# Expert stage of a hybrid encoder block: place of the scales' copy, of the one-hots and of the first weight splits

## The chip, the cores and the metric

One core of one Trainium2 chip. The time is device microseconds of one execution. TensorE multiplies, VectorE and ScalarE work on elements, GpSimd does as well and issues indirect transfers, SyncE issues the weight loads; each of them works through its own instructions in a fixed order.

## The reference

One layer over 1024 tokens of 1024 channels: windowed attention and gated linear attention, then an expert layer, then a gated embedding and a last norm. The change touches the expert layer alone:

```python
def expert_choice_ffn(xn, w_router, w_gate, w_up, w_down):
    B, S, D = xn.shape
    cap = CAPACITY_FACTOR * S // N_EXPERTS
    aff = jax.nn.softmax(jnp.einsum('bsd,de->bse', xn, w_router).astype(jnp.float32), axis=-1)
    top_aff, top_idx = lax.top_k(jnp.swapaxes(aff, 1, 2), cap)
    bidx = jnp.arange(B)[:, None, None]
    xg = xn[bidx, top_idx]
    hid = jax.nn.silu(jnp.einsum('becd,edf->becf', xg, w_gate)) * jnp.einsum('becd,edf->becf', xg, w_up)
    y = jnp.einsum('becf,efd->becd', hid, w_down) * top_aff[..., None].astype(xn.dtype)
    return jnp.zeros((B, S, D), dtype=y.dtype).at[bidx, top_idx].add(y)
```

16 experts, each takes its 128 best tokens of 1024 and runs them through three matrices of 1024x1024 in float32: 12 MB of weights per expert.

## The kernel before

Every product is made of three: a float32 is split into a high part (a cast to float32r on ScalarE) and a low part (what the cast left, a subtraction on VectorE), and TensorE adds high x high, high x low and low x high (`split`, line 105, and the three matmuls at lines 1198 to 1200).

Before the experts come a router and a sort. For each of the eight token tiles, affinities to the 16 experts are computed; VectorE finds the 128 largest of every expert with max and replace steps (lines 916, 918) and merges sorted halves with pairs of max and min (lines 935, 936). From the threshold follows `posT`, each token's place among the expert's 128.

`tokens(e)` (line 1119) turns the places into a list: VectorE compares `posT` with a row of numbers, which gives the one-hots `oh` (line 1121), TensorE multiplies them with the token numbers (line 1125), VectorE adds two columns into `idx` (line 1127). `gather(e)` has GpSimd issue an indirect transfer that brings the 128 rows of `xn_d` into `xg` (line 1133); each row carries 1024 normed channels and 17 scales (16 affinities and the norm's factor). There is one buffer `xg`.

`begin(e)` copies the scales of `xg` into `col` on ScalarE (line 1214) and has TensorE turn the rows, two groups of four transposes (line 1178), which are split into `xt_h` and `xt_l`. `gate`, `up` and `down` each consist of four quarters (`quarter_of`): a piece of 1 MB of weights arrives in one of 15 raw buffers, is split into `hi` and `lo` (called `slot` in the profile; three pairs of buffers in all), and is multiplied by 12 matmuls. `gate` ends with a SiLU on ScalarE (line 1229), `up` with a product on VectorE (line 1238), both scaled by `col`; `down` ends with `y`, scaled on ScalarE (line 1255), which GpSimd adds to `h_d` with an indirect transfer (line 1256).

The experts are staggered: while expert e goes through gate and up, the hidden rows of e − 1 are turned inside its gate (`hidden_turned`), and the down product of e − 1 comes after its up. After the first quarter of that down, `ahead(e + 1)` begins expert e + 1, gathers e + 2 and finds the list of e + 3. Before the loop, lists 0, 1 and 2 and the gathers 0 and 1 are written down first. The first two pieces have their lo half made by GpSimd; their splits are put behind an instruction of the lists, `found`, and one of the router, `placed`, each on its own engine.

The order of work on each engine comes from the program's scheduler, which starts from the order of writing and moves instructions by its own estimate of when they are ready. Three things bind it: data and buffers; `on_pe`, which keeps the transposes and expert products of TensorE in the order of writing (the products with one-hots are not bound so); and `tc.issue_after(ins)`, which puts what is written in its block behind `ins` on the engine of `ins`.

## Time and profile before

| | us |
|---|---|
| median of 3 runs | 1800.95 (1798.8 to 1804.61) |
| profiled execution | 1803.04, its span 1801.3 |
| TensorE busy in the span | 1676.5 (93%) |
| VectorE busy | 1207.0 (67%) |
| ScalarE busy | 898.5 (50%) |
| GpSimd busy | 204.4 (11%) |
| of these, line 106 on weight pieces (`slot`): VectorE, the lo halves | 433.0 |
| line 106 on weight pieces: ScalarE, the hi halves | 373.9 |

The sort and the lists reach to about 1050 us of the span, the experts from there to about 1680, and the last part to its end. A row of a timeline gives start, length, engine, line, operation, output and inputs, and in brackets how long the engine had been idle and what ended that. A matmul's row overlaps with the next one's, so twelve of 0.39 us take less than twelve times that.

### The profile page before, as it was taken

What the parts mean: (1) busy time and instruction counts of PE and PEld (TensorE: products, weight loads), DVE (VectorE), ACT (ScalarE), POOL (GpSimd) and SP (SyncE); (2) the same over time, 40 slices, a digit from 0 to 9 for tenths busy, and PEclk for the clock granted to TensorE, in tenths of its full rate; (3) what the DMA queues carried; (4) which work ended last, traced back from release to release, by engine and by line L of the source; (5) the groups of instructions that cost most, each with busy time, mean ns of one, the idle gap of its engine ahead of it and who ended that gap; (6) DMA issues with size and microseconds to landing.
All of it is one profiled execution on the core that took longest, in us unless ns stands there. A gap on an engine that the chain in (4) does not pass through costs nothing.

```text
span 1801.3 us, 23090 instructions
## 1 busy us (share of the span) xinstructions
PE 1676.5 (93%) x8795; PEld 1370.3 (76%) x8795; DVE 1207.0 (67%) x2254; ACT 898.5 (50%) x1259; POOL 204.4 (11%) x199
## 2 busy tenths in 40 slices
PE   7998999999999999999988769999999998889997
PEld 6977766768898989888866557777777776677786
DVE  7446754633746473743577968888888887778575
ACT  4345555432626262530322336777677776667642
POOL 1013300000000000000143310111111111101000
PEclk9999999999999999999988979999999999999999
DMA  6032410524221211164423869999999998882811
GB/s 223 1 101 106 129 47 24 164 69 153 61 68 51 71 48 47 51 230 143 174 94 118 320 244 359 354 369 376 377 347 365 372 358 325 315 308 93 291 47 47
DMA packets 123607, 335.06 MB, mean 186 GB/s; under 512 B 9180, under 2 KB 41988, under 8 KB 123496
## 3 DMA queue, kind: packets, MB, share of 16 engines
q1 hardware_dynamic: 106784, 277.96, 42.7%
q0 software_dynamic: 14704, 53.17, 8.7%
q10 hardware_dynamic: 2008, 2.46, 0.4%
q8 instruction: 69, 1.13, 0.3%
q14 instruction: 42, 0.34, 0.1%
HBM read 290.50 MB, written 43.06 MB: 185 GB/s over the span
## 4 chain that ended last, share of the span: by engine, by line
PE 56%; issue 26%; DVE 9%; POOL 3%; DMA 3%; ACT 2%; DVEq 0%; POOLq 0%; SPq 0%; ACTq 0%
PE ps_mm L111 12%; PE ps_mm L109 11%; PE ps_mm L110 11%; PE ps_b L109 2%; PE ps_b L111 2%; PE ps_b L110 2%; POOL h_d L1256 2%; POOL xg L1133 1%; DMA xg<-xn_d,idx 1%; PE ps_b L1199 1%; DVE rs_y L133 1%; PE ps_b L1200 1%; PE ps_b L1198 1%; PE ps_a L533 1%; PE ps_tr L562 1%
## 5 line engine op out<-in xcount | busy, mean ns | idle before, releaser
L106 DVE TENSOR_TENSOR slot<-slot 128x2048 fp32r<-128x2048 f32 (+1 forms) x191 | 433.0, 2284 | 108.0 <-ACT slot L106 105.1
L106 ACT CAST slot<-slot 128x2048 fp32r<-128x2048 f32 (+1 forms) x200 | 373.9, 1875 | 118.4 <-PE ps_b L1199 44.6
L111 PE MATMUL ps_mm<-aT_h,wl 128*128 128x512 f32 x512 | 204.4, 399 | 0.0
L109 PE MATMUL ps_mm<-aT_h,wh 128*128 128x512 f32 x512 | 203.1, 397 | 1.2 <-ACT sgr L246 1.2
L110 PE MATMUL ps_mm<-aT_l,wh 128*128 128x512 f32 x512 | 203.8, 398 | 0.0
L1199 PE MATMUL ps_b<-slot,xt_h 128*128 128x512 f32 x256 | 103.3, 403 | 15.0 <-DVE slot L106 15.0
L1199 PE MATMUL ps_mm<-slot,xt_h 128*128 128x512 f32 x256 | 102.7, 401 | 13.6 <-DVE slot L106 13.6
L109 PEld LDWEIGHTS ps_mm<-aT_h,wh 128*128 128x128 f32 x512 | 97.4, 190 | 18.8 <-ACT sgr L246 1.5
L111 PEld LDWEIGHTS ps_mm<-aT_h,wl 128*128 128x128 f32 x512 | 97.5, 190 | 18.3 <-issue 1.2
L110 PEld LDWEIGHTS ps_mm<-aT_l,wh 128*128 128x128 f32 x512 | 97.2, 190 | 18.4 <-issue 1.2
L1198 PE MATMUL ps_mm<-slot,xt_h 128*128 128x512 f32 x256 | 103.3, 404 | 5.3 <-ACT slot L106 3.9
L1198 PE MATMUL ps_b<-slot,xt_h 128*128 128x512 f32 x256 | 102.8, 402 | 5.5 <-ACT slot L106 5.5
L106 DVE TENSOR_TENSOR wl<-raw,wh 128x2048 fp32r<-128x2048 f32 (+1 forms) x29 | 61.5, 2122 | 65.0 <-ACT wh L106 65.0
L1200 PE MATMUL ps_b<-slot,xt_l 128*128 128x512 f32 x256 | 102.0, 398 | 0.0
L1200 PE MATMUL ps_mm<-slot,xt_l 128*128 128x512 f32 x256 | 101.5, 396 | 0.0
L106 ACT CAST wh<-raw 128x2048 fp32r<-128x2048 f32 (+1 forms) x30 | 52.0, 1735 | 93.5 <-PE ps_mm L110 88.7
L109 PE MATMUL ps_mm<-wh,aT_h 128*128 128x256 f32 x320 | 91.7, 287 | 0.8 <-DVE sgr L588 0.8
L111 PE MATMUL ps_mm<-wh,aT_l 128*128 128x256 f32 x320 | 90.6, 283 | 1.6 <-DVE aT_l L106 1.6
L110 PE MATMUL ps_mm<-wl,aT_h 128*128 128x256 f32 x320 | 90.7, 284 | 0.0
L109 PE MATMUL ps_mm<-slot 128*128 128x512 f32 x192 | 80.1, 417 | 0.0
L111 PE MATMUL ps_mm<-slot 128*128 128x512 f32 x192 | 77.8, 405 | 0.0
L110 PE MATMUL ps_mm<-slot 128*128 128x512 f32 x192 | 77.5, 404 | 0.0
(392 smaller groups left out, 3924.7 us busy)
## 6 DMA issues: line engine op xcount, KB each, us to landing
slot<-in_w_exp_gate_dram SPq DMA_DIRECT2D x64, 1024.0 KB, 7.9
slot<-in_w_exp_down_dram SPq DMA_DIRECT2D x64, 1024.0 KB, 7.6
slot<-in_w_exp_up_dram SPq DMA_DIRECT2D x60, 1024.0 KB, 5.7
raw<-in_w_in_dram SPq DMA_DIRECT2D x16, 1024.0 KB, 6.8
raw<-in_w_in_dram SPq DMA_DIRECT2D x14, 512.0 KB, 5.3
sg_d<-sgr POOLq DMA_DIRECT2D x14, 512.0 KB, 2.9
xn_d<-xa POOLq DMA_DIRECT2D x8, 520.5 KB, 3.8
xt<-in_x_dram SPq DMA_DIRECT2D x8, 512.0 KB, 7.0
```

The lines of the kernel that those rows point to most:

```text
L106: return nc.scalar.copy(hi, src), eng.tensor_sub(lo, src, hi)
L109: nc.tensor.matmul(out_ps, sh, mh, start=start, stop=False)
L110: nc.tensor.matmul(out_ps, sh, ml, start=False, stop=False)
L111: nc.tensor.matmul(out_ps, sl, mh, start=False, stop=stop)
L133: eng.scalar_tensor_tensor(y, t, c, y, op0=ALU.add, op1=ALU.mult)
L533: nc.tensor.matmul(pss[g][:, 0:n], qhl[r, g, hc], kT_l[r, ks], start=False, stop=False)
L562: nc.tensor.transpose(pt[:, o:o + 128], sm[g][c][:, j * 128:(j + 1) * 128], ident)
L1133: return nc.gpsimd.indirect_dma_start(out=xg, out_offset=None, in_=xn_d[:, :], in_offset=bass.IndirectOffsetOnAxis(ap=st[e]["idx"][:, 0:1] ...
L1198: on_pe(nc.tensor.matmul(po[c], src[0][:, kk], hi[:, k, cc], start=first, stop=False))
L1199: on_pe(nc.tensor.matmul(po[c], src[0][:, kk], lo[:, k, cc], start=False, stop=False))
L1200: on_pe(nc.tensor.matmul(po[c], src[1][:, kk], hi[:, k, cc], start=False, stop=last))
L1256: nc.gpsimd.indirect_dma_start(out=h_d[:, :], in_=y, in_offset=None, compute_op=ALU.add, out_offset=bass.IndirectOffsetOnAxis(ap=s["idx"][ ...
```

## The change

`begin` writes the copy of scales behind the splits of the turned rows, and puts it behind the second cast on ScalarE. The lists and the gather of expert 1 and the list of expert 2 are written behind the first quarter of the first gate, the list of expert 1 behind the first piece's lo half on VectorE. From expert 1 on, the list of e + 2 is written after the second quarter of the up product of e. Expert 1 is begun after the third quarter of the first up product. The last hidden rows are turned inside the down product of expert 14. The lo halves of the first pieces are made by VectorE, and the first three pieces (before: two) have their splits behind `found` and `placed`; `found` is now the index of expert 0 (before: of expert 1).

```diff
@@ -1134,12 +1134,8 @@
             out=xg, out_offset=None, in_=xn_d[:, :],
             in_offset=bass.IndirectOffsetOnAxis(ap=st[e]["idx"][:, 0:1], axis=0)).ins
 
-    for e in range(2):
-        found = tokens(e)
-        if e == 0:
-            gathered = gather(0)
-    gather(1)
-    tokens(2)
+    found = tokens(0)
+    gathered = gather(0)
 
 
     for i in range(4):
@@ -1177,7 +1173,7 @@
         for c in range(4):
             on_pe(nc.tensor.transpose(pt[:, c * 128:(c + 1) * 128],
                                       src[:, (g * 4 + c) * 128:(g * 4 + c + 1) * 128], ident))
-        split(th[:, g * 4:g * 4 + 4], tl[:, g * 4:g * 4 + 4], pt.rearrange("p (c t) -> p c t", c=4))
+        return split(th[:, g * 4:g * 4 + 4], tl[:, g * 4:g * 4 + 4], pt.rearrange("p (c t) -> p c t", c=4))
 
     def quarter_of(po, src, w, q):
 
@@ -1186,10 +1182,10 @@
             raw = loaded(next_pool(), (2, D), w[q * 256:q * 256 + 256], nc.gpsimd if 12 <= n < 16 else nc.sync)
         hi, lo = [slot(rawE if n % 3 == 2 else whl, (2, D), F32R) for _ in range(2)]
         with ExitStack() as es:
-            if n < 2:
+            if n < 3:
                 for ins in (found, placed):
                     es.enter_context(tc.issue_after(ins))
-            split(hi, lo, raw, nc.gpsimd if n < 2 else nc.vector)
+            lo_ins[0] = split(hi, lo, raw)[1].ins
         for k in range(2):
             kk = 2 * q + k
             for c in range(2):
@@ -1202,7 +1198,7 @@
     def hl_pair(po, name, **kw):
         return [po.tile([128, KC, 128], F32R, name=name + x, **kw) for x in ("_h", "_l")]
 
-    n_banks = [0]
+    n_banks, lo_ins = [0], [None]
 
     def two_banks():
         n_banks[0] += 1
@@ -1211,9 +1207,11 @@
     def begin(e):
         st[e]["xt"] = hl_pair(e2, "xt")
         col = st[e]["col"] = eg.tile([128, NE + 1], F32, name="col", bufs=NE)
-        nc.scalar.copy(col, st[e]["xg"][:, D:TW])
         for g in range(2):
-            turned(st[e]["xg"], *st[e]["xt"], g, "a")
+            here, _ = turned(st[e]["xg"], *st[e]["xt"], g, "a")
+
+        with tc.issue_after(here.ins):
+            nc.scalar.copy(col, st[e]["xg"][:, D:TW])
 
     def gate(e, after):
 
@@ -1228,11 +1226,13 @@
             cc = slice(c * 512, c * 512 + 512)
             nc.scalar.activation(s["hid"][:, cc], pg[c], AF.Silu, scale=s["col"][:, NE:NE + 1])
 
-    def up(e):
+    def up(e, after):
         s = st[e]
         pu = two_banks()
         for q in range(4):
             quarter_of(pu, s["xt"], w_eu[e], q)
+            if q in after:
+                after[q]()
         for c in range(2):
             cc = slice(c * 512, c * 512 + 512)
             nc.vector.scalar_tensor_tensor(s["hid"][:, cc], pu[c], s["col"][:, NE:NE + 1], s["hid"][:, cc],
@@ -1256,24 +1256,30 @@
         nc.gpsimd.indirect_dma_start(out=h_d[:, :], in_=y, in_offset=None, compute_op=ALU.add,
                                      out_offset=bass.IndirectOffsetOnAxis(ap=s["idx"][:, 0:1], axis=0))
 
+    def tokens_of(e, after=None):
+        if e < NE:
+            with tc.issue_after(after) if after else ExitStack():
+                tokens(e)
+
     def ahead(e):
 
         if e < NE:
             begin(e)
         if e + 1 < NE:
             gather(e + 1)
-        if e + 2 < NE:
-            tokens(e + 2)
+
+    def first_tokens():
+        tokens_of(1, lo_ins[0])
+        gather(1)
+        tokens_of(2)
 
     begin(0)
     for e in range(NE):
-        gate(e, {1: partial(hidden_turned, e - 1)} if e else {})
-        up(e)
+        last = {1: partial(hidden_turned, e)} if e == NE - 1 else {}
+        gate(e, {1: partial(hidden_turned, e - 1)} if e else {0: first_tokens})
+        up(e, {1: partial(tokens_of, e + 2)} if e else {2: partial(ahead, 1)})
         if e:
-            down(e - 1, {0: partial(ahead, e + 1)})
-        else:
-            ahead(1)
-    hidden_turned(NE - 1)
+            down(e - 1, {0: partial(ahead, e + 1), **last})
     down(NE - 1, {})
 
 
```

How that moves instructions, at three places. ScalarE around the start of an expert in the middle of the stage; `slot` is the hi half of a weight piece, `xt_h` the turned rows, `y` the result of the down product of another expert. Before:

```order
L106 CAST slot<-slot 128x2048 x5
L106 CAST xt_h<-ps_a 128x512 x2
L106 CAST slot<-slot 128x2048
L1214 COPY col<-xg 128x17
L106 CAST slot<-slot 128x2048
L1255 ACTIVATE y<-ps_mm,col 128x512
L106 CAST slot<-slot 128x2048
L1255 ACTIVATE y<-ps_mm,col 128x512
L106 CAST slot<-slot 128x2048 x2
```

After:

```order
L106 CAST slot<-slot 128x2048 x5
L106 CAST xt_h<-ps_a 128x512 x2
L1214 COPY col<-xg 128x17
L106 CAST slot<-slot 128x2048 x2
L1255 ACTIVATE y<-ps_b,col 128x512
L106 CAST slot<-slot 128x2048
L1255 ACTIVATE y<-ps_b,col 128x512
L106 CAST slot<-slot 128x2048 x2
L106 CAST hT_h<-ps_tr 128x512 x2
```

The copy stood one piece behind the casts of the turned rows, and it was the copy for the expert after, whose rows had just been asked for; now it stands right behind the casts and reads the rows that these casts came from.

VectorE at the end of the sort, from the places to the first expert's rows; `oh` and `idx` are one-hots and list of an expert, `slot` here is the lo half of a weight piece. Before:

```order
L1114 TENSOR_TENSOR posT<-sl_9694,sl_9695 128x128
L1121 TENSOR_TENSOR oh<-posT,iot 128x1024
L1127 TENSOR_SCALAR idx<-ps_a 128x1
L1121 TENSOR_TENSOR oh<-posT,iot 128x1024
L1127 TENSOR_SCALAR idx<-ps_a 128x1
L1121 TENSOR_TENSOR oh<-posT,iot 128x1024
L1127 TENSOR_SCALAR idx<-ps_a 128x1
L1121 TENSOR_TENSOR oh<-posT,iot 128x1024
L106 TENSOR_TENSOR xt_l<-ps_a,xt_h 128x512 x2
L106 TENSOR_TENSOR slot<-slot 128x2048 x7
```

After:

```order
L1114 TENSOR_TENSOR posT<-sl_9694,sl_9695 128x128
L1121 TENSOR_TENSOR oh<-posT,iot 128x1024
L1127 TENSOR_SCALAR idx<-ps_a 128x1
L106 TENSOR_TENSOR slot<-slot 128x2048
L1121 TENSOR_TENSOR oh<-posT,iot 128x1024
L106 TENSOR_TENSOR slot<-slot 128x2048
L106 TENSOR_TENSOR xt_l<-ps_a,xt_h 128x512
L106 TENSOR_TENSOR slot<-slot 128x2048
L106 TENSOR_TENSOR xt_l<-ps_a,xt_h 128x512
L1127 TENSOR_SCALAR idx<-ps_a 128x1
L1121 TENSOR_TENSOR oh<-posT,iot 128x1024
L106 TENSOR_TENSOR slot<-slot 128x2048
```

Behind the first list there stood two more lists and a one-hot, and the lo halves of pieces 0 to 2 had been made elsewhere; now these three halves stand between the lists and the two low parts of the turned rows.

GpSimd at the same place; `slot` at line 106 is the lo half of a piece, at line 813 the load of a piece of the second up product. Before:

```order
L1052 DMA xn_d<-xa 128x1041
L106 TENSOR_TENSOR slot<-slot 128x2048 x2
L1133 DMA xg<-xn_d,idx 128x1041
L813 DMA slot<-in_w_exp_up_dram 128x2x1024
L1133 DMA xg<-xn_d,idx 128x1041
L813 DMA slot<-in_w_exp_up_dram 128x2x1024 x3
```

After:

```order
L1052 DMA xn_d<-xa 128x1041
L1133 DMA xg<-xn_d,idx 128x1041
L813 DMA slot<-in_w_exp_up_dram 128x2x1024 x3
L1133 DMA xg<-xn_d,idx 128x1041
L813 DMA slot<-in_w_exp_up_dram 128x2x1024
```

The two lo halves ahead of the first gather are gone, and three loads instead of one stand between the first gather and the second.

## Rows read from the trace of the kernel before

**Rows 1.** Busy time of each engine in four stretches of the experts: two single microseconds, and two stretches that reach from one expert's scatter to the next. The columns: start and end in us, length, engine busy times as "engine busy (xcount)", then the granted TensorE clock as a share of full speed, the mean busy share of the DMA engines, and GB/s.
```profile
1171.00:1172.00 1.00, 1.00 (x6) 0.84 (x5) 0.93 (x1) 0.65 (x3) 0.00 (x0) 1.00 1.04 238
1177.00:1178.00 1.00, 1.00 (x7) 0.80 (x6) 1.00 (x1) 0.72 (x1) 0.00 (x0) 1.00 1.05 430
1200.76:1237.65 36.89, 35.11 (x170) 28.71 (x169) 32.12 (x21) 27.11 (x22) 4.75 (x2) 1.00 0.98 370
1543.68:1586.73 43.05, 37.37 (x161) 30.01 (x161) 30.89 (x19) 26.86 (x22) 4.92 (x3) 0.94 0.87 318
```

**Rows 2.** Groups of instructions by line in the stretch from 1110 to 1600 us: TensorE's products of an expert's rows, and then ScalarE's copy of gathered scales. Behind the bar: busy time and mean of one, then idle time of the engine just ahead of the group's instructions, and what ended it.
```profile
L1199 PE MATMUL ps_b<-slot,xt_h 128*128 128x512 f32 x208 | 84.3, 405 | 13.3 <-DVE slot L106 13.3
L1198 PE MATMUL ps_b<-slot,xt_h 128*128 128x512 f32 x208 | 84.1, 404 | 5.5 <-ACT slot L106 5.5
...
L1198 PE MATMUL ps_mm<-slot,xt_h 128*128 128x512 f32 x192 | 77.4, 403 | 3.9 <-ACT slot L106 3.9
L1199 PE MATMUL ps_mm<-slot,xt_h 128*128 128x512 f32 x192 | 77.2, 402 | 11.6 <-DVE slot L106 11.6
...
L1214 ACT COPY col<-xg 128x17 f32<-128x17 f32 x13 | 2.7, 207 | 66.4 <-DMA xg<-xn_d,idx 66.4
```

**Rows 3.** Timeline of ScalarE from 1187 us on. The columns: start, length in us, instruction, and in brackets the idle time of its engine ahead of it and what ended it.
```profile
1187.25 1.06 ACT L106 CAST xt_h<-ps_a 128x512 fp32r<-128x512 f32 x2
1189.05 1.91 ACT L106 CAST slot<-slot 128x2048 fp32r<-128x2048 f32 x1 [0.74 <-PE ps_mm L1199]
1195.52 0.21 ACT L1214 COPY col<-xg 128x17 f32<-128x17 f32 x1 [4.55 <-DMA xg<-xn_d,idx]
```

**Rows 4.** Timeline of VectorE in the same stretch, columns as before.
```profile
1191.21 2.28 DVE L106 TENSOR_TENSOR slot<-slot 128x2048 fp32r<-128x2048 f32 x1
1193.41 1.22 DVE L1121 TENSOR_TENSOR oh<-posT,iot 128x1024 bf16<-128x1024 bf16 x1
1197.56 9.26 DVE L106 TENSOR_TENSOR slot<-slot 128x2048 fp32r<-128x2048 f32 x4 [2.94 <-ACT slot L106]
```

**Rows 5.** Timeline of TensorE in the same stretch: its one row that has idle time ahead of it.
```profile
1199.91 0.50 PE L1199 MATMUL ps_b<-slot,xt_h 128*128 128x512 f32 x1 [1.82 <-DVE slot L106]
```

**Rows 6.** Timelines of ScalarE (first row) and TensorE in a late expert, 1530 to 1565 us: the rows with the long waits.
```profile
1538.44 0.21 ACT L1214 COPY col<-xg 128x17 f32<-128x17 f32 x1 [6.99 <-DMA xg<-xn_d,idx]
...
1540.50 0.80 PE L1198 MATMUL ps_mm<-slot,xt_h 128*128 128x512 f32 x1 [2.41 <-ACT slot L106]
...
1542.82 0.79 PE L1199 MATMUL ps_mm<-slot,xt_h 128*128 128x512 f32 x1 [1.53 <-DVE slot L106]
...
1560.94 0.50 PE L1199 MATMUL ps_b<-slot,xt_h 128*128 128x512 f32 x1 [1.28 <-DVE slot L106]
```

**Rows 7.** Timelines of VectorE and GpSimd while the top 128 tokens are sorted out, 1003 to 1034 us.
```profile
1003.70 2.27 DVE L106 TENSOR_TENSOR slot<-slot 128x2048 fp32r<-128x2048 f32 x1
1005.90 0.14 DVE L1038 RECIPROCAL rd<-den 128x1 f32<-128x1 f32 x1
...
1023.98 9.02 POOL L106 TENSOR_TENSOR slot<-slot 128x2048 fp32r<-128x2048 f32 x2 [4.33 <-PE ps_b L110]
...
1024.24 4.38 DVE L935 TENSOR_TENSOR top<-top 16x64 f32<-16x64 f32 x1
1028.55 4.53 DVE L936 TENSOR_TENSOR top<-top 16x64 f32<-16x64 f32 x1
...
1033.20 0.20 DVE L935 TENSOR_TENSOR top<-top 16x64 f32<-16x64 f32 x1
```

**Rows 8.** Timeline of all engines from the index of expert 0 to its turned rows, 1049 to 1058 us: VectorE and GpSimd.
```profile
1049.26 0.22 DVE L1127 TENSOR_SCALAR idx<-ps_a 128x1 int32<-128x1 f32 x1 [0.47 <-PE ps_a L1125]
...
1049.77 1.76 POOL L1133 DMA_INDIRECT xg<-xn_d,idx  x1 [16.78 <-DVE idx L1127]
...
1051.52 0.76 POOL L813 DMA_DIRECT2D slot<-in_w_exp_up_dram  x1
...
1056.78 1.50 DVE L106 TENSOR_TENSOR xt_l<-ps_a,xt_h 128x512 fp32r<-128x512 f32 x2 [2.51 <-ACT xt_h L106]
```

**Rows 9.** Timelines of TensorE and VectorE at the turning of expert 1 (first row), and at the last hidden product and the last down product.
```profile
1082.89 0.50 PE L1198 MATMUL ps_mm<-slot,xt_h 128*128 128x512 f32 x1 [1.37 <-ACT xt_h L106]
...
1648.21 1.43 DVE L1238 SCALAR_TENSOR_TENSOR hid<-ps_b,col,hid 128x512 f32<-128x512 f32 x2 [0.75 <-PE ps_b L1200]
...
1663.09 0.76 PE L1198 MATMUL ps_b<-slot,hT_h 128*128 128x512 f32 x1 [2.07 <-ACT hT_h L106]
...
1664.95 0.79 PE L1200 MATMUL ps_b<-slot,hT_l 128*128 128x512 f32 x1 [0.68 <-DVE hT_l L106]
```

**Rows 10.** Busy time of each engine in the six stretches inside the experts in which the granted clock is low; columns as in rows 1.
```profile
1311.00:1315.00 4.00, 4.00 (x11) 3.13 (x12) 3.91 (x2) 2.35 (x2) 2.91 (x1) 0.57 0.75 259
1424.00:1428.00 4.00, 4.00 (x15) 3.17 (x14) 3.78 (x2) 2.57 (x2) 2.91 (x1) 0.57 0.88 323
1499.00:1503.00 4.00, 3.47 (x9) 2.75 (x10) 3.73 (x3) 2.91 (x3) 2.61 (x1) 0.57 0.61 185
1540.00:1547.00 7.00, 4.97 (x11) 3.59 (x12) 6.26 (x3) 5.20 (x5) 2.74 (x1) 0.52 0.44 161
1584.00:1592.00 8.00, 6.18 (x16) 4.85 (x16) 6.30 (x3) 5.71 (x5) 2.74 (x1) 0.57 0.64 216
1663.00:1670.00 7.00, 6.24 (x14) 4.45 (x15) 4.69 (x4) 3.13 (x4) 2.72 (x1) 0.51 0.62 189
```

## The prediction

> **What bounds the kernel now.** I read the busy times by stretch first, then who waited for whom, then the timelines of single engines where TensorE stands still. Over one whole expert, from one scatter to the next (36.89 us), TensorE is busy 35.11 us, VectorE 32.12, ScalarE 27.11, and the share of the DMA engines reads 0.98 [rows 1]. So TensorE needs 35.1 us and is kept waiting 1.8; VectorE and DMA come close behind. The groups by line say where the 1.8 come from. In a stretch that holds 13 copies of gathered scales, ScalarE stands 66.4 us ahead of these copies, each waiting for a transfer of rows that had only just been asked for [rows 2]. One case in order of time: after the casts of the turned rows and one weight piece, the copy waits 4.55 us for its gather [rows 3]; the next hi cast stands behind it; VectorE has no lo half to make and idles 2.94 us [rows 4]; TensorE, which had a piece or two in hand, stops 1.82 us for that lo half [rows 5]. The copied scales are wanted by nobody for most of an expert's time. In the late experts the same wait is 6.99 us long and TensorE stops twice, 2.41 and 1.53 us [rows 6].
>
> Ahead of the experts the bound is VectorE, which finds the top 128 tokens of every expert. There two tiny operations (16x64) that take 0.20 us elsewhere last 4.38 and 4.53 us, exactly while GpSimd makes the lo halves of the first two weight pieces (9.02 us for both); and 2.27 us of the same chain go to the lo half of a third piece [rows 7]. TensorE has nothing to do at the end of it and waits for the index of expert 0.
>
> **The change, term by term.**
>
> *A, the first pieces.* GpSimd's two splits go, and the third split moves from the middle of the sort to behind the index of expert 0. By the starts of the next rows, the third split costs 1005.90 − 1003.70 = 2.2 us, and the two stretched operations take from 1024.24 to 1033.20, 8.96 us in place of some 0.4: 8.6 [rows 7]. I take VectorE as without a break here, so its chain gets shorter by 2.2 + 8.6 = 10.8 us. Bounds: 8 (the 2.2 turn into a wait for the last token tile, whose router runs on TensorE and ScalarE meanwhile) and 11. The lo halves now stand behind the index: split, one-hot, split, then the first turned low part, 2.3 + 1.2 + 2.3 = 5.8 us [rows 4]. Their cover is the gather of expert 0 and its turning: index at 1049.26, low part of the rows begun at 1056.78, 7.5 us [rows 8]. So they cost nothing; without the cover they would cost 5.8. The third split and the second low part come after that, while TensorE works through pieces 0 and 1, some 5 us. Three weight loads now stand on GpSimd's queue between the first gather and the second; one took 0.76 us to issue [rows 8], so gather 1 is put back about 2 us, and it has until the end of the up product. I take 10.8.
>
> *B, expert 1 turned inside the up product of expert 0* instead of behind it. It removes a stop of 1.37 us [rows 9], but VectorE's order now has half of the hidden product ahead of the turned low part, so some of the stop stays: 1.0, bounds 0 and 2.
>
> *C, the copy behind the turned rows.* The copy now reads rows that TensorE has already read, so it waits for nothing, and itself takes 0.21 us [rows 3]. In the stretch of rows 2 TensorE stood 13.3 + 5.5 + 3.9 + 11.6 = 34.3 us for hi and lo halves. Two stops of about 1.28 us of another kind are in it (the one at 1560.94 stands for them [rows 6]): there a cast waits behind the SiLU, ScalarE's order keeps that pattern in the last four experts, and I leave those. 34.3 − 2.6 = 31.7; I take 31. On top comes the clock. Five stretches inside the experts have a granted clock of 0.52 to 0.57, at the 1.2 GHz level for most of their length, and each begins at one of these stops (those of rows 6 for one); busy time times the missing share gives 4.00 x 0.43 twice, 3.47 x 0.43, 4.97 x 0.48 and 6.18 x 0.43, 10.0 us together [rows 10]. After the 1.28 us stops no such stretch begins. So C is 41; bounds 22 (DMA, below) and 43.
>
> *D, the last hidden rows* are turned inside the down product of expert 14, no longer behind it. Now TensorE waits 2.07 and 0.68 us there [rows 9], and the stretch has a clock of 0.51 over 6.24 us busy, 3.1 us [rows 10]: 5.8 together. The hidden product is there 0.75 + 1.43 us after the up product's end [rows 9], and the turning comes two pieces later, some 5 us. I take 5, bounds 2 and 6.
>
> *E, the one-hots in the up product.* A one-hot (1.22 us) and its index (0.21) leave the place behind the turned rows, where VectorE idled anyway on account of the copy [rows 4], and stand in front of the first down piece. Same work, but now without that cover. VectorE's spare time is 35.1 − 32.1 = 3 us per expert; a piece lasts 35.1/12 = 2.9 us on TensorE and 9.26/4 = 2.3 on VectorE, so it wins back at most 0.6 per piece, and 1.4 us in one place leave it late for two or three pieces. I expect hardly a stop: 0.15 us per expert, 2 in all, bounds 0 and 14. The index is found an expert later than before, but still ahead of the release of the row buffer, for which the gather waits anyway.
>
> Sum against the profiled execution (1803.0 us, of which the span is 1801.3): 10.8 + 1 + 41 + 5 − 2 = 55.8, so 1747.2. That execution lies 2.1 us above the median of the runs shown (1800.95); on the median I forecast 1800.95 − 55.8 = **1745 us**.
>
> **Rivals.**
>
> *DMA takes the place of the wait.* For it: a share of 0.98 over 36.89 us, taken at its word, is 36.2 us an expert, 1.1 more than TensorE needs, and 14 experts give 15 us back: 1760. Harder still, 370 GB/s is the most that transfers hold over a whole expert, so all periods stay at 36.89 and only the three long ones (43.05) fall to it: 18.5 in place of 41, nothing for E, 1803.0 − 35.3 − 2.1 = 1766. Against: in single microseconds the share reads 1.04 and 1.05 and 430 GB/s are moved where no indirect transfer runs [rows 1], so the need is nearer 0.98/1.04 x 36.89 = 34.8 us; the engines pause where no buffer has come free, which is just when TensorE stands; and 15 raw buffers are a lead of over an expert, which a lack of 1.1 us per expert eats up before it stops anybody. The Trainium skill has a rule for the hard form: "SBUF — State Buffer", section "A bandwidth-pool intuition that's wrong (but worth ruling out)", puts HBM at about 358 GB/s for a core and calls it almost always the end-to-end bottleneck. By that figure an estimate for the 370 GB/s x 36.89 us that an expert moves is 38 us, more than its period now, and C would bring nothing in the early experts; the trace disagrees, since 370 GB/s are held over a whole period.
>
> *VectorE takes it.* It has little room, and the one-hot lost its cover. If TensorE stops 0.75 us once per expert, 14 experts cost 10 us: 1755. For it: lo halves are made only a piece or two ahead, since three pairs of buffers hold the halves. Against: after the waits of now VectorE makes four halves in a row (9.26 us [rows 4]) and TensorE stops no second time.
>
> *The change doesn't do at the sort what it says:* the stretched operations have another cause than GpSimd's splits. Then A is 2.2 and the time 1754. Against: two splits, two stretched operations, and both over when GpSimd is.
>
> *Slower: gathers come too late.* The turning waits on TensorE's own row for the gathered rows, with everything behind it, and the gather is now released only after transposes, casts and copy of the expert before (1 + 1.06 + 0.21 us [rows 3], with waits 3). That leaves 32 of 35 us. Now the copy meets its rows after waits of 4.55 and at worst 6.99 us [rows 3, 6]. Landings later than 32 us after the issue would cost; to end above the time of now, each of 14 experts must lose 4.4 us more than it gains, landings of 36 us: 1810. Nothing in the trace comes near.
>
> **How the numbers follow.** Forecast 1745 (1734 to 1752): 0.62. VectorE, 1755: 0.16. DMA, 1760: 0.07, and its hard form, 1766: 0.04. Sort unchanged, 1754: 0.06. Late gathers, 1810: 0.02. The other 0.03 lie to both sides. The low end, 1734, is A 11, B 2, C 43, D 6, E 0 and the four late stops gone as well (5 us); the high end, 1763, lies half way between the two forms of the DMA rival and leaves out the hard one and the late gathers. About 0.3% (5 us) is what a measurement of this kernel can tell from no change: faster 0.97, within 0.01, slower 0.02.
>
> **What would show it.** A: no operation of 16x64 above 1 us, and the first gather near 1039 us. C: no wait of the copy for a transfer, periods near 35 us for most experts and 36 for the last four, no clock stretches between. If periods stay above 36 with the DMA share at 1.0, it was DMA; if TensorE stops for lo halves right behind the one-hots, VectorE. D: the last down product starts without a stop. The forecast is most wrong if the stops of C are replaced one for one by others.

## The result, and the profile after

The changed kernel takes **1741.18 us** (median of 4 runs, 1740.73 to 1741.50) against 1802.78 us (4 runs, 1798.8 to 1807.01) for the kernel before on the same chip: a ratio of 0.966, 95% interval 0.963 to 0.968. That is 61.6 us less, where 55.8 were forecast. The profiled execution took 1741.5 us, of which the span is 1739.8. Where the time went, by the starts of the index of expert 0 and of the scatters in the two traces (us):

| stretch of the span | before | after | difference | forecast |
|---|---|---|---|---|
| to the index of expert 0 | 1049.26 | 1039.15 | -10.1 | A: -10.8 |
| from there to the first scatter | 76.32 | 72.95 | -3.4 | B: -1.0, a stop of C |
| first to 15th scatter | 537.25 | 494.37 | -42.9 | C and E: -39 |
| 15th to last scatter | 16.19 | 11.39 | -4.8 | D: -5 |
| behind it | 122.3 | 121.9 | -0.3 | 0 |

Busy times by stretch answer to [rows 1]: two periods of middle experts, one of the last four (a period reaches from one scatter to the next). The columns are those of [rows 1].
```profile
1146.91:1181.72 34.81, 34.81 (x170) 28.80 (x169) 32.12 (x21) 27.35 (x22) 5.05 (x2) 1.00 1.02 383
1390.60:1425.41 34.81, 34.81 (x170) 28.80 (x169) 32.11 (x21) 27.34 (x22) 5.04 (x2) 1.00 1.03 390
1496.39:1532.53 36.14, 34.80 (x162) 28.62 (x161) 31.47 (x19) 27.19 (x22) 3.85 (x3) 1.00 1.02 392
```
Read length against the PE column: in the middle experts TensorE is busy for the whole period. It sets the pace; VectorE has 2.7 us to spare, and the transfers, at a share of 1.02, hold nobody up. In the late expert 1.34 us of TensorE are left idle. Groups by line, which answer to [rows 2], first of ScalarE from 1110 to 1550 us, with the copy:
```profile
L106 ACT CAST slot<-slot 128x2048 fp32r<-128x2048 f32 x150 | 286.6, 1913 | 73.2 <-PE ps_b L1195 36.0 <-PE ps_mm L1195 34.6 <-DVE oh L1121 1.2
...
L1214 ACT COPY col<-xg 128x17 f32<-128x17 f32 x12 | 2.6, 218 | 0.0
```
and of TensorE from 1075 to 1600 us:
```profile
L1195 PE MATMUL ps_b<-slot,xt_h 128*128 128x512 f32 x240 | 93.8, 391 | 3.4 <-DVE slot L106 3.4
L1196 PE MATMUL ps_mm<-slot,xt_l 128*128 128x512 f32 x240 | 93.7, 390 | 0.5 <-DVE xt_l L106 0.5
...
L1195 PE MATMUL ps_mm<-slot,xt_h 128*128 128x512 f32 x239 | 93.3, 390 | 2.7 <-DVE slot L106 2.7
```
The copy waits for nothing, and what ends ScalarE's idle time now is TensorE giving buffers back: ScalarE is ahead of TensorE, not behind it. TensorE's 34 us of stops [rows 2] have become 6.6. The granted clock is 1.00 over the whole of 1075 to 1600 us, so the low stretches of [rows 10] inside the experts are gone too. The sort answers to [rows 7] in a view of one tile (durations min/median/max in ns):
```profile
L935 DVE TENSOR_TENSOR top<-top x14: 194/200/205, 1009.3 to 1025.2; 16x64 f32<-16x64 f32 x14
L936 DVE TENSOR_TENSOR top<-top x14: 205/206/210, 1009.4 to 1025.3; 16x64 f32<-16x64 f32 x14
```
None of these is above 0.21 us. From the index of expert 0 to its turned rows, the timeline of all engines (to set beside [rows 8]):
```profile
1039.15 0.22 DVE L1127 TENSOR_SCALAR idx<-ps_a 128x1 int32<-128x1 f32 x1 [0.47 <-PE ps_a L1125]
1039.29 2.28 DVE L106 TENSOR_TENSOR slot<-slot 128x2048 fp32r<-128x2048 f32 x1
1039.67 2.82 POOL L1133 DMA_INDIRECT xg<-xn_d,idx  x1 [20.21 <-DVE idx L1127]
1041.49 1.22 DVE L1121 TENSOR_TENSOR oh<-posT,iot 128x1024 bf16<-128x1024 bf16 x1
1042.48 2.21 POOL L813 DMA_DIRECT2D slot<-in_w_exp_up_dram  x3
1042.62 2.28 DVE L106 TENSOR_TENSOR slot<-slot 128x2048 fp32r<-128x2048 f32 x1
...
1046.07 1.94 PE L1174 MATMUL ps_a<-ident,xg 128*128 128x128 f32 x8 [6.96 <-DMA xg<-xn_d,idx]
...
1047.86 0.69 DVE L106 TENSOR_TENSOR xt_l<-ps_a,xt_h 128x512 fp32r<-128x512 f32 x1 [2.95 <-ACT xt_h L106]
```
The lo halves are covered, since VectorE still idles 2.95 us before the turned rows. But the gather takes 2.82 us to issue in place of 1.76, and TensorE turns its rows 6.4 us after the issue began, where it was 5.2 (1054.99 for the transposes of before): of the 10.1 us won ahead, 8.9 reach the first product. The stops that are left, TensorE's rows with idle time ahead of them:
```profile
1073.42 0.50 PE L1194 MATMUL ps_mm<-slot,xt_h 128*128 128x512 f32 x1 [0.45 <-ACT xt_h L106]
1074.70 0.50 PE L1196 MATMUL ps_mm<-slot,xt_l 128*128 128x512 f32 x1 [0.55 <-DVE xt_l L106]
...
1458.86 0.50 PE L1195 MATMUL ps_b<-slot,xt_h 128*128 128x512 f32 x1 [0.77 <-DVE slot L106]
...
1474.99 0.50 PE L1195 MATMUL ps_mm<-slot,xt_h 128*128 128x512 f32 x1 [1.34 <-DVE slot L106]
...
1604.59 0.50 PE L1194 MATMUL ps_b<-slot,hT_h 128*128 128x512 f32 x1 [0.45 <-ACT hT_h L106]
...
1606.13 0.50 PE L1196 MATMUL ps_b<-slot,hT_l 128*128 128x512 f32 x1 [0.80 <-DVE hT_l L106]
```
The first two are what is left of the stop of 1.37 us at the turning of expert 1, the last two of those of 2.07 and 0.68 us at the last down product [rows 9]. The one at 1474.99 stands for four, one in each of experts 12 to 15. None lies between 1075 and 1458 us.

### The profile page after: what moved, and what is told of

The parts are those of the page before. It is cut to its first block, busy times and chain, and to the rows that moved or that the text cites. A ratio compares the mean times of both kernels' runs of the same rounds, so it can differ in the third digit from the quotient of the medians.

```text
span 1739.8 us, 23112 instructions
## 1 busy us (share of the span) xinstructions
PE 1658.0 (95%) x8795; PEld 1361.8 (78%) x8795; DVE 1201.4 (69%) x2256; ACT 902.2 (52%) x1259; POOL 196.4 (11%) x197
## 3 DMA queue, kind: packets, MB, share of 16 engines
q8 instruction: 69, 1.13, 0.3%
## 5 line engine op out<-in xcount | busy, mean ns | idle before, releaser
L106 DVE TENSOR_TENSOR slot<-slot 128x2048 fp32r<-128x2048 f32 (+1 forms) x193 | 438.0, 2283 | 52.7 <-ACT slot L106 50.2
L110 PEld LDWEIGHTS ps_mm<-aT_l,wh 128*128 128x128 f32 x512 | 97.3, 190 | 18.5 <-issue 1.2
L1195 PE MATMUL ps_b<-slot,xt_h 128*128 128x512 f32 x256 | 100.1, 391 | 4.0 <-DVE slot L106 4.0
L1195 PE MATMUL ps_mm<-slot,xt_h 128*128 128x512 f32 x256 | 100.2, 392 | 2.7 <-DVE slot L106 2.7
L1194 PE MATMUL ps_mm<-slot,xt_h 128*128 128x512 f32 x256 | 101.5, 396 | 0.5 <-ACT xt_h L106 0.5
L1194 PE MATMUL ps_b<-slot,xt_h 128*128 128x512 f32 x256 | 101.0, 395 | 0.0
```

The lines of the kernel that those rows point to most:

```text
L106: return nc.scalar.copy(hi, src), eng.tensor_sub(lo, src, hi)
L110: nc.tensor.matmul(out_ps, sh, ml, start=False, stop=False)
L1194: on_pe(nc.tensor.matmul(po[c], src[0][:, kk], hi[:, k, cc], start=first, stop=False))
L1195: on_pe(nc.tensor.matmul(po[c], src[0][:, kk], lo[:, k, cc], start=False, stop=False))
```

## Experiments

Eleven kernels were run. Times are medians; the kernel before ran beside them at 1802.87 to 1803.05 us. The first starts from the kernel before, the last two from the kernel of run 9, the others from the kernel after.

**1. The copy alone** (on the kernel before).
```
-        nc.scalar.copy(col, st[e]["xg"][:, D:TW])
         for g in range(2):
-            turned(st[e]["xg"], *st[e]["xt"], g, "a")
+            here, _ = turned(st[e]["xg"], *st[e]["xt"], g, "a")
+        with tc.issue_after(here.ins):
+            nc.scalar.copy(col, st[e]["xg"][:, D:TW])
```


> The kernel before, with one thing of the change: the copy of the gathered scales stands behind the second cast of the turned rows. Theory (the copy's place is the large term, and it stands alone): the stops of 1.8 and 1.5 us per expert go, the low-clock stretches inside the experts go, the distance between scatters falls from 36.9 to about 34.8 us, and the time to 1755 to 1763 us (1802.8 less 40 to 47). Rival 1 (the transfers bind next): the distance stays at 36 us or more and the time at 1780 or above. Rival 2 (the one-hots, still beside the turned rows here, hold VectorE up once the stops are gone): a stop of 0.5 to 1 us per expert behind VectorE, 1765 to 1775 us.

Measured: 1754.34 us, ratio 0.972 (0.969 to 0.976), a little below the theory's range. One period of a middle expert:
```profile
1227.71:1262.52 34.81, 34.81 (x169) 28.80 (x169) 32.16 (x21) 27.32 (x22) 5.05 (x3) 1.00 1.03 393
```
With the copy moved and nothing else, TensorE is busy all the time. Both rivals fall: the transfers run at the same 1.03, and the one-hots beside the turned rows stop nobody.

**2. Everything but the copy.**
```
+        nc.scalar.copy(col, st[e]["xg"][:, D:TW])
         for g in range(2):
-            here, _ = turned(st[e]["xg"], *st[e]["xt"], g, "a")
-        with tc.issue_after(here.ins):
-            nc.scalar.copy(col, st[e]["xg"][:, D:TW])
+            turned(st[e]["xg"], *st[e]["xt"], g, "a")
```


> The kernel after, with the copy written ahead of the turned rows again. Theory: all but the copy's term stays; the stops behind ScalarE are back in each of the middle experts, the distance between scatters is about 36.9 us, and the time 1782 to 1788 us (1741.2 and 41 to 47). Rival (the one-hots' new place had taken the pressure off ScalarE's queue, so that much of the gain is theirs): 1765 us or less.

Measured: 1793.03 us, ratio 0.995 (0.992 to 0.997). Timeline of ScalarE, and of TensorE behind it:
```profile
1227.10 0.21 ACT L1210 COPY col<-xg 128x17 f32<-128x17 f32 x1 [4.60 <-DMA xg<-xn_d,idx]
...
1231.49 0.50 PE L1195 MATMUL ps_mm<-slot,xt_h 128*128 128x512 f32 x1 [1.82 <-DVE slot L106]
```
The wait and the stop of [rows 3, 5] are back, in nearly every expert, and the time is 5 us above the end of what was expected. First to 15th scatter takes 540.9 us, 3.6 more than before. So the copy is worth 48.7 us alone and 51.9 with the rest; the rest is worth 10.0 without it. They add up: 48.7 + 10.0 = 58.7 of 61.6.

**3. An early copy that ScalarE need not wait for.**
```
+        nc.gpsimd.tensor_copy(col, st[e]["xg"][:, D:TW])
         for g in range(2):
-            here, _ = turned(st[e]["xg"], *st[e]["xt"], g, "a")
-        with tc.issue_after(here.ins):
-            nc.scalar.copy(col, st[e]["xg"][:, D:TW])
+            turned(st[e]["xg"], *st[e]["xt"], g, "a")
```


> The kernel after, with the copy of the scales ahead of the turned rows again, but on GpSimd, whose queue holds only gathers, scatters and a few early loads. Theory (what cost 50 us was that the copy's wait for the gather held up ScalarE's queue behind it, not where the copy stands among the reads of the gathered rows): within 4 us of the kernel after, 1738 to 1745 us, no stop between experts 1 and 10. Rival (an early copy costs wherever it runs, for instance since the next gather or the SiLU then waits for it): 1760 us or more.

Measured: 1740.16 us, ratio 0.965 (0.963 to 0.966), the same as the kernel after. The copy stands early and waits as ever, but on GpSimd:
```profile
1213.68 0.82 POOL L1210 COPY col<-xg 128x17 f32<-128x17 f32 x1 [6.64 <-DMA xg<-xn_d,idx]
```
A wait of 6.64 us costs nothing there. It was not the copy and not its place, but a wait for a transfer in the queue in which the casts stand.

**4. The first two lo halves on GpSimd again.**
```
-            lo_ins[0] = split(hi, lo, raw)[1].ins
+            lo_ins[0] = split(hi, lo, raw, nc.gpsimd if n < 2 else nc.vector)[1].ins
```


> The kernel after, with the low halves of the first two pieces on GpSimd again. Theory (two GpSimd subtractions of 9 us stretch the VectorE operations of the sort's end that run beside them): the two operations of 4.4 us are back in the sort's end, the index of expert 0 comes 8 to 9 us later (near 1047.7 us of the span instead of 1039.15), and the time is 1748 to 1751 us. Rival (the sort's gain came from the third split's place alone): the index comes within 1 us of 1039.15 and the time is 1740 to 1743. On the slower gather of expert 0 (issue 2.82 us, PE starts 6.4 us after it): if VectorE's subtractions beside it slowed it, its issue falls to 1.8 us or less here, and PE starts some 5.2 us after it; if the three weight loads behind it did, it stays at 2.8 and 6.4.

Measured: 1748.54 us, ratio 0.968 (0.964 to 0.972), index at 1049.73: 10.6 us later than in the kernel after, of which 1.4 lie ahead of the last step on the affinities (1006.58 here, 1005.22 there) and 9.2 behind it, where 8 to 9 were expected. GpSimd's two splits, and the VectorE operations beside them:
```profile
1022.84 4.64 POOL L106 TENSOR_TENSOR slot<-slot 128x2048 fp32r<-128x2048 f32 x1 [1.46 <-ACT slot L106]
1028.82 4.51 POOL L106 TENSOR_TENSOR slot<-slot 128x2048 fp32r<-128x2048 f32 x1 [1.33 <-ACT slot L106]
```
```profile
1023.05 4.51 DVE L935 TENSOR_TENSOR srt<-hs 16x64 f32<-16x64 f32 x1
...
1028.85 4.56 DVE L935 TENSOR_TENSOR top<-top 16x64 f32<-16x64 f32 x1
```
Two splits, two stretched operations, each begun just behind the start of one and over when it is. It is not the pair of operations of before; whichever of the maxima and minima of two SBUF arrays comes next on VectorE is held. This is what the Trainium skill says in "SBUF — State Buffer", section "Who interferes with whom": a VectorE instruction with two SBUF inputs contends with a GpSimd instruction that reads SBUF. The trace agrees, with 4.5 us in place of 0.2. The gather of expert 0 shows the reverse side:
```profile
1050.24 1.75 POOL L1133 DMA_INDIRECT xg<-xn_d,idx  x1 [16.91 <-DVE idx L1127]
1051.01 2.28 DVE L106 TENSOR_TENSOR slot<-slot 128x2048 fp32r<-128x2048 f32 x1
1051.99 2.21 POOL L813 DMA_DIRECT2D slot<-in_w_exp_up_dram  x3
...
1055.52 1.94 PE L1174 MATMUL ps_a<-ident,xg 128*128 128x128 f32 x8 [5.82 <-DMA xg<-xn_d,idx]
```
With fewer VectorE splits beside it, its issue is back at 1.75 us and TensorE starts 5.3 us behind it, though the three loads still follow it.

**5. The early loads on SP's queue.**
```
-            raw = loaded(next_pool(), (2, D), w[q * 256:q * 256 + 256], nc.gpsimd if 12 <= n < 16 else nc.sync)
+            raw = loaded(next_pool(), (2, D), w[q * 256:q * 256 + 256], nc.sync)
```


> The kernel after, with the four early pieces that GpSimd loads put on SP's queue. If VectorE's subtractions made the gather of expert 0 slower: its issue stays at 2.8 us and PE starts 6.4 us after it began. If the weight loads right behind it did: 1.8 us or less and 5.3 us. Gather 1 has nothing ahead of it on GpSimd now but still waits for its index: it starts within 0.5 us of 1052.7 us if the index sets it, 2 us earlier if the loads did.

Measured: 1741.16 us (one run). The gather in the timeline of GpSimd, and its transposes in that of TensorE:
```profile
1036.77 2.83 POOL L1133 DMA_INDIRECT xg<-xn_d,idx  x1 [20.22 <-DVE idx L1127]
...
1046.29 1.94 PE L1174 MATMUL ps_a<-ident,xg 128*128 128x128 f32 x8 [10.06 <-DMA xg<-xn_d,idx]
```
The issue stays at 2.83 us with no load behind it, so VectorE's work beside it is the cause. What neither theory had: TensorE now starts 9.5 us behind the issue, not 6.4. The four loads no longer stand behind the gather, and TensorE gets its rows 3 us later. From the issue to the transposes the share of the DMA engines is 1.03 at 411 GB/s here and 0.45 at 141 GB/s in the kernel after, so the gather now shares engines that are full; that this alone makes the 3 us was not tested. Gather 1 starts at 1053.66, 1.0 us behind its index (1052.67), as it does in the kernel after (1052.74 and 1051.75): the index sets it, not the loads.

**6. The third split free to stand in the sort.**
```
-            if n < 3:
+            if n < 2:
```


> The kernel after, with the third piece's low half free to stand where its data allows, so that VectorE does it inside the sort again. Theory (the prediction's 2.2 us for it): counted from the first step of the merges the sort is no longer, but its start, and the index of expert 0, come 2.2 us later, near 1041.4 us (runs so far differ by 1.5 us before the sort's start), and the split stands ahead of the merges in VectorE's rows. Rival (VectorE has idle time there that takes it in): the index within 1 us of 1039.2 to 1040.3.

Measured: 1742.68 us (one run), index at 1038.44, so by the index the rival is right. But the start of the sort differs from run to run by more than that (last section), so the step of the sort that holds the split is compared: from VectorE's last operation on one token tile's affinities to that on the next it is 1004.28 - 987.96 = 16.32 us here, as in the kernel before (1006.56 - 990.24), and 1005.22 - 990.69 = 14.53 in the kernel after. The split stands there again, as VectorE's timeline shows, and costs 1.8 us:
```profile
1001.42 2.27 DVE L106 TENSOR_TENSOR slot<-slot 128x2048 fp32r<-128x2048 f32 x1
```

**7. The one-hots where they were.**
```
             gather(e + 1)
+        if e + 2 < NE:
+            tokens(e + 2)
...
-        up(e, {1: partial(tokens_of, e + 2)} if e else {2: partial(ahead, 1)})
+        up(e, {} if e else {2: partial(ahead, 1)})
```


> The kernel after, with the index of the later experts worked out where it was before (behind the gather in the down product, not in the up product). Theory (the one-hot's place costs and gives nothing, since VectorE has 2.7 us idle in each 34.8): 1739 to 1744 us. Rival (beside the turned rows the one-hot of 1.2 us holds the low half of a piece up): a stop of 0.5 to 1 us in each of 12 experts, 1747 to 1753 us.

Measured: 1740.45 us, ratio 0.964 (0.960 to 0.968); first to 15th scatter 494.64 us against 494.37. The place of the one-hots is worth nothing either way.

**8. The last hidden rows turned behind the down product of expert 14.**
```
-            down(e - 1, {0: partial(ahead, e + 1), **last})
+            down(e - 1, {0: partial(ahead, e + 1)})
+    hidden_turned(NE - 1)
     down(NE - 1, {})
```


> The kernel after, with the hidden rows of expert 15 turned behind the down product of expert 14 again. Theory (their value is the two stops alone, 3.2 us behind against 1.25 us in front, as the runs with and without it show): the stops are 2.07 and 1.13 us, 1742.5 to 1744.5 us. Rival (the 5 us of the prediction, of which half is the clock at its lower level in the last product): a low-clock stretch of 6 us is back in the last product, 1745.5 us or more.

Measured: 1744.85 us, ratio 0.968 (0.966 to 0.970), which lies between the two ranges, so the trace has to decide. The stops are 2.07 and 0.64 us. Busy times over the start of the last down product:
```profile
1604.20:1611.00 6.80, 6.16 (x15) 4.33 (x16) 4.40 (x4) 2.93 (x3) 2.43 (x1) 0.52 0.65 204
```
A granted clock of 0.52 is back, and from the 15th to the last scatter it is 16.10 us against 11.39. The theory falls, and the prediction's account, stops and clock, stands. In run 1 the same late turning had stops of 2.07 and 1.13 us and no clock stretch there, and took 13.83 us: what such stops cost depends on whether the clock falls behind them. Why it fell in one and not in the other stays open.

**9. SiLU behind the casts.** In experts 12 to 15 of the kernel after, the cast of the second up piece stands behind a SiLU that waits for the gate product's end, as ScalarE's timeline shows for expert 12:
```profile
1470.12 0.69 ACT L1227 ACTIVATE hid<-ps_b,col 128x512 f32<-128x512 f32 x1 [2.39 <-PE ps_b L1196]
1470.71 1.90 ACT L106 CAST slot<-slot 128x2048 fp32r<-128x2048 f32 x1
```
Its lo half comes behind that cast, and TensorE stops for it at 1474.99 (above). This kernel holds ScalarE's order fixed:
```
+        def silu(c):
             cc = slice(c * 512, c * 512 + 512)
+            with tc.issue_after(hi_ins[0]):
                 nc.scalar.activation(s["hid"][:, cc], pg[c], AF.Silu, scale=s["col"][:, NE:NE + 1])
...
+        up(e, {1: partial(behind_casts, silu, 0, e), 2: partial(behind_casts, silu, 1, e)})
```


> The kernel after, with each expert's two SiLU written behind the high halves of the second and third up pieces (ScalarE's order of the early experts, now in the last five too). Theory (the four stops of 1.33 us that are left in experts 12 to 15 come from the cast of the second up piece standing behind a SiLU that waits for the gate product's end): the four go, and perhaps the one of 0.77 us; 1734 to 1737 us (1741.2 less 5.3 to 6.1). Rival (in those experts a piece is cast one place later throughout, so the stop moves to the next product): stops of 1 us or more elsewhere in experts 12 to 15, 1739 us or more.

Measured: **1732.93 us**, ratio 0.961 (0.959 to 0.963), faster than the kernel after. The same place of expert 13 as ScalarE has it now, and the period behind it:
```profile
1501.38 3.90 ACT L106 CAST slot<-slot 128x2048 fp32r<-128x2048 f32 x2
1505.63 0.69 ACT L1229 ACTIVATE hid<-ps_mm,col 128x512 f32<-128x512 f32 x1 [0.35 <-PE ps_mm L1197]
```
```profile
1495.45:1529.97 34.52, 34.52 (x162) 28.72 (x161) 31.48 (x19) 27.45 (x22) 3.86 (x3) 1.00 1.03 395
```
Two casts ahead of the SiLU, and TensorE busy for the whole of the period. The four stops are gone. Against them stands one new stop of 0.54 us at 1443.58, and the one of 0.77 us stays; first to 15th scatter takes 488.7 us, 5.7 less. The two profiled executions differ by 5.0 us (1736.47 and 1741.5), the medians by 8.2: the rest is spread between executions of this kernel (1731.04 to 1736.89), of which the profiled one is among the longest.

**10. SiLU behind the casts, and the one-hots where they were** (on the kernel of run 9).
```
             gather(e + 1)
+        if e + 2 < NE:
+            tokens(e + 2)
...
-        if c == 0 and e:
-            tokens_of(e + 2)
```


> The SiLU behind the casts, and the index of the later experts worked out behind the gather as before the change. Theory (of the two VectorE stops left in the run with the SiLU behind the casts, 0.54 and 0.77 us, the second goes with the one-hot's place, as in the run that moved the one-hots alone): 1731 to 1734 us, the same as with the SiLU alone within what a measurement tells. Rival (in the old place the one-hot now meets the casts of the last five experts): new stops of 0.5 us or more in each of experts 12 to 15, 1735 us or more.

Measured: 1732.88 us, ratio 0.961 (0.959 to 0.962), the same as run 9. No stop is left between 1075 and 1594 us; first to 15th scatter takes 488.2 us.

**11. More transfers** (on the kernel of run 9).
```
+                if e > 2:
+                    with tc.issue_after(last_load[0]):
+                        nc.sync.dma_start(x_d, w_eg[e][0:128])
```


> The kernel with the SiLU behind the casts, and one copy more per expert, of 0.5 MB from the gate weights to a scratch array in device memory (0.5 MB read and 0.5 MB written, for experts 3 to 15); its output is not used. It is read against the run with the SiLU behind the casts. Theory (TensorE alone sets the distance between scatters, the transfers have room although their packets' time is 1.02 of the span): at most 5 us more, distance 34.8 to 35.2 us. Rival (the transfers are full, and the next microsecond taken from TensorE would bring nothing): 1.05 MB more at some 400 GB/s is 2.6 us per expert, 25 to 32 us more, with stops of TensorE behind the casts that wait for loads.

Measured: 1737.09 us, ratio 0.963 (0.961 to 0.965), 4.2 us more than run 9. A period with the copy in it, then the transfer queue's view of six experts without and with it (median us from issue to landing at the end):
```profile
1181.15:1215.96 34.81, 34.81 (x170) 28.80 (x169) 32.12 (x21) 27.34 (x22) 5.03 (x2) 1.00 1.03 399
```
```profile
slot<-in_w_exp_gate_dram SPq DMA_DIRECT2D x24, 1024.0 KB, 7.7
```
```profile
slot<-in_w_exp_gate_dram SPq DMA_DIRECT2D x24, 1024.0 KB, 11.8
...
x_d<-in_w_exp_gate_dram SPq DMA_DIRECT2D x6, 512.0 KB, 13.3
```
Over these six experts loads land 4 us later, and the period stays at 34.81 us. In time, and over these periods, the theory is right. That the transfers have room does not follow, and a closer look at the trace says they have little. Over the first six periods (208.87 us in both kernels) they move 399 GB/s with the copy and 394 without. The copy asks for 0.5 MB in 34.81 us (as the trace counts a copy's packets), which is 15 GB/s, and only 5 more came. The rest shows as delay: taken in stretches of 35 us from 1110 to 1320 us, the gate loads' median from issue to landing is 7.5, 9.0, 9.4, 11.4, 12.2 and 13.8 us. Without the copy it stays between 7.4 and 8.4 from 1110 to 1425 us. So with the copy the transfers are full, as the rival says, and the lead of the buffers takes the lack; the rival's price is wrong since it left that lead out. No cast waits for a load between 1110 and 1550 us.

The stops that came (0.55 and four of 0.77 us, all behind VectorE, between 1338 and 1463 us) are of the kind of those that run 9 has at 1443.58 and 1459.53: ScalarE's rows ahead of the first are the same in both, and the pattern begins three experts earlier. That the build ordered it so on account of the copy is likely and not shown. From 1354 to 1462 us they make the periods 35.9 us, and from there the landing times fall (12.3, 11.7, 11.6 us).

## Why the prediction was right, and where its sizes were off

*A, forecast 10.8 us.* Measured ahead of the index: 1.8 for the third split (run 6, taken as 2.2), and 42.70 - 33.93 = 8.8 from the end of that step to the index (1006.56 to 1049.26 before, 1005.22 to 1039.15 after; taken as 8.6). The last operation of that step, before and after:
```profile
1006.56 0.21 DVE L1039 TENSOR_SCALAR affA<-affA,rd 128x16 f32<-128x16 f32 x1
```
```profile
1005.22 0.21 DVE L1039 TENSOR_SCALAR affA<-affA,rd 128x16 f32<-128x16 f32 x1
```
The cause holds: run 4 brings stretched operations back with GpSimd's splits. What was missing is that VectorE's splits beside the first gather lengthen its issue from 1.76 to 2.82 us (runs 4 and 5): A is worth 9.4 at the first product, not 10.8. That the loads behind the gather put gather 1 back was wrong (run 5), and cost the forecast nothing.

*B, forecast 1.0.* Two stops of 0.45 and 0.55 us are left of 1.37. From the index to the first scatter run 1 takes 72.46 us; the kernel after, 72.95, of which 1.2 are the gather's, so B is 0.7. That is a difference between two kernels; no run has B alone.

*C, forecast 41.* The mechanism is shown from both sides (runs 1 and 2), and run 3 shows it to be the wait in ScalarE's queue. The size was too small. In run 1 the way from the index to the last scatter is 49.7 us shorter. TensorE's stops of over 0.35 us there, from the first product on, fall from 41.3 us in 26 to 10.4 in 8: 30.9. The clock gives 10.0, and 3.1 more at the last product [rows 10]. That leaves 5.7 us, and the term that was short is the price of a stop. TensorE's timeline of before around the stop of 1.78 us:
```profile
1234.63 0.39 PE L1198 MATMUL ps_mm<-slot,xt_h 128*128 128x512 f32 x1
1236.80 0.50 PE L1199 MATMUL ps_mm<-slot,xt_h 128*128 128x512 f32 x1 [1.78 <-DVE slot L106]
1237.14 0.40 PE L1200 MATMUL ps_mm<-slot,xt_l 128*128 128x512 f32 x1
```
Matmuls follow each other every 0.23 us. From 1234.63 to 1237.14 two steps should take 0.46 and take 2.51: 2.05 us are lost, 0.27 more than the idle time that the row lists, since the ones on either side no longer overlap. The two periods say the same: 36.89 - 34.81 = 2.08 with one stop of 1.78. The prediction read the busy 35.11 us [rows 1] as TensorE's need, in which this 0.3 was hidden. At 18 stops fewer, 0.27 each is 4.9 of the 5.7 us. The four late stops stayed as foreseen, at 1.33 us; run 9 shows their cause.

*D, forecast 5.* Between the last two scatters 4.8 us are gained, and 4.7 are lost when the change is undone (run 8). Stops of 0.45 and 0.80 us are left, where none was foreseen.

*E, forecast a cost of 2.* No cost can be seen (run 7). One stop, that of 0.77 us at 1458.86, is not there with the one-hots in their old place.

So the terms were off by little in A, B and D, E's cost was not there, and C was too small by some 6 us: the forecast erred low on the gain, and no two large errors had to cancel.

Of the rivals, DMA falls with periods at TensorE's own length in which loads land as soon as before (by stretches of 35 us the median of the gate loads stays between 7.4 and 8.0 us from 1110 to 1425 us of the kernel after; it was 8.5 before). It falls narrowly: with 399 GB/s as the most that a whole period moved (run 11) and 394 used without the extra copy, an estimate of what the transfers need is 394/399 x 34.81 = 34.4 us, 0.4 less than TensorE. The prediction's 370 GB/s as the most that a whole period holds was too low, since that period was set by the stops. The rule of the Trainium skill ("SBUF — State Buffer", section "A bandwidth-pool intuition that's wrong (but worth ruling out)", some 358 GB/s for a core and the bottleneck) is contradicted by 383 to 399 GB/s over whole periods in which TensorE never stands. The hard form also counted three periods of 43.05 us; by the scatters of before there are two near it (43.29 and 43.05) and one of 38.86, so its 18.5 us should be 14.5. VectorE falls with no stop from 1075 to 1458 us, the late gathers with a copy and transposes that wait for no transfer there. That the sort would not change falls with run 4.

## What to carry to other kernels

An instruction that waits for a transfer belongs behind one that has waited for the same data already, or on a queue that has nothing urgent behind it; its own length (0.2 us here) says nothing about its price. A stop of a pipelined engine costs its listed idle time and the overlap on both sides (0.27 us here), so take the need of an engine from a period in which it does not stop, not from its busy time in one in which it does. Where the order of a queue is left to the build, look at late repetitions of a loop too: the same code had another order from expert 12 on, for 1.3 us in each. And when an experiment adds load to transfers that run ahead of their use, look at the landing times as well as at the period: a lack goes into the lead first.

## What the runs showed beside

- A GpSimd instruction of 4.5 us that reads SBUF holds a VectorE maximum or minimum of two SBUF arrays, 0.2 us by itself, until it is over (run 4). In the other direction VectorE's subtractions and one-hots stretch what GpSimd needs to issue a gather: 0.98 us at the shortest, 1.75 and 1.76 with less of them beside it, 2.82 and 2.83 with splits and a one-hot all the way.
- The share of the DMA engines reads 1.02 to 1.03 over a whole period both where the transfers just keep up (383 to 394 GB/s, landing times the same from period to period) and where they do not (399 GB/s, landing times up from 7.5 to 13.8 us in six periods, run 11). What tells the two apart is the landing times.
- The merges of the sort start at 1006.1 to 1013.3 us in these kernels, though little before them differs. Between the same two points TensorE did the same 493 matmuls in 108 us in run 6 (880 to 988 us) and in 111 us in the kernel after (880 to 991), with a mean granted clock of 0.95 and 0.91 and busy for 92.4 and 95.9 us. So a little more time at the clock's lower level, in a stage where TensorE often waits, moves all that follows by some 3 us; differences of that size are read from points inside the trace, not from the end. What makes the clock fall there in some kernels and not in others stays open.
